# Index-add over 32 batches: one staged batch behind each of the first five groups, and shared DMA semaphores

## The chip, the cores and the metric

The kernel runs on one core of a Trainium2 chip. The metric is the device time of one execution in microseconds. Before the change it is 84.39 us, the median of 3 runs (83.99 to 84.44). A change of about 0.5% is what such runs can tell from none.

## The reference

For each of 32 batches, 128 rows of `source` are added to rows of `x` that `indices` names. An index can occur several times in a batch, and then all its rows are added.

```python
batch, seq, dim = 32, 512, 256          # x: 32 x 512 x 256, f32
num_updates = 128                       # indices: 32 x 128, source: 32 x 128 x 256
result = x.copy()
for b in range(batch):
    for i in range(num_updates):
        result[b, indices[b, i]] += source[b, i]
```

## The kernel before

The batches are treated in eight groups of four (`GB = 4`), and in two ways.

**Direct batches**, 0 to 24. The whole batch of `x` is copied from HBM to HBM into `out` (`copy`, L117; four copies are issued by ScalarE, 21 by SyncE). GpSimd gathers the 128 rows of `x` that the indices name into `got` (`gather`, L459). TensorE multiplies the source rows by a matrix that says which updates have equal indices (`same`), so that each of the 128 rows of `add` in PSUM holds the full sum for its index (`sums`, L380 and L389). VectorE adds this to the gathered rows (L400), and GpSimd scatters them over the copy in `out` (`scatter`, L473). So that a repeated index is written once, `masks` (L288 to L361) works out for each update whether an earlier one has the same index; `to_i` (L361) is the row to write, or a number out of bounds, which the scatter skips. Gathers from batch 12 on (`SKIP_FROM`) also use `to_i`, and wait for it; the first twelve use `row_i`, which is ready earlier.

**Staged batches**, 25 to 31. The batch of `x` is loaded into SBUF (`load_x`, L136). In `staged_batch` VectorE makes a one-hot matrix (L407), TensorE spreads the source rows over all 512 rows of the batch in two halves (L421), VectorE adds each half to the loaded rows (L431), and SyncE stores the whole batch (L493).

**What sets the order.** Nothing is scheduled by a planner: each engine runs its instructions in the order in which they are written, and waits on semaphores. VectorE and TensorE get their work from one loop, which alternates `sums(g)`, `masks(g + 4)` and, from g = 2 on, one staged batch, after `masks(0)` to `masks(3)`:

```python
        for g in range(NG):
            sums(g)
            if g + MASKS_AHEAD < NG:
                masks(g + MASKS_AHEAD)
            if g >= 2:
                staged_batch(later.pop(0))
```

The staged batches are taken in the order 28, 29, 30, 31, 25, 26, 27. Groups 0 to 5 multiply in blocks of 32 rows, 16 matmuls a group; group 6 has one direct batch, and group 7 none, so `sums(7)` does nothing. A staged batch is two one-hot halves of two matmuls each. The profile counts every f32 matmul as two, so it shows 32 for a group's sums and 8 for a staged batch. `add` is a single buffer in PSUM, so `sums(g)` on TensorE waits for VectorE's L400 of the group before; `bc` and `spread` have two buffers each.

GpSimd's queue holds all 25 gathers in the order of batches, and behind them all 25 scatters in the same order. SyncE's queue holds the loads and copies in one fixed mixture (`LOADS`, `SRC_ORDER`), and behind them the seven stores, each waiting for its batch. Then it waits for all stores and all scatters, and the kernel ends.

**Semaphores.** Every direct batch has one for its copy (`s_copy`, waited for by its scatter) and one for its gather (`s_got`, waited for by the L400 of its group, four waits in a row).

Of the kernel before, what the change touches and what calls it, by code (L numbers as in the profile page):

```python
# [10 lines left out]
GB = 4  # L11
COPY_ROWS = 32
WIDE = 6
STAGED = (25, 26, 27, 28, 29, 30, 31)
MASKS_AHEAD = 4
SKIP_FROM = 12
# [3 lines left out]
def kernel(  # L20
# [18 lines left out]
    _, NU = indices.shape  # L39
# [3 lines left out]
    R = P // GB  # L43
    DIRECT = [b for b in range(B) if b not in STAGED]
    N_DIRECT = len(DIRECT)
    assert DIRECT[: WIDE * GB] == list(range(WIDE * GB))

# [14 lines left out]
    ident = sb.tile([B, B], f32)  # L62
    ident_r = sb.tile([B, WIDE * GB, R], f32)
    of_group = sb.tile([B, NG], f32)
# [14 lines left out]
    src = [sb.tile([P, GB, D], f32, name=f"src{g}") for g in range(NG)]  # L79
    got = [sb.tile([P, GB, D], f32, name=f"got{g}") for g in range(WIDE + 1)]  # L80
    same = [sb.tile([P, GB, P], f32, name=f"same{g}") for g in range(NG)]
    same_n = [sb.tile([P, GB, P], f32, name=f"same_n{k}") for k in range(2)]
    earlier = [sb.tile([P, GB, P], f32, name=f"earlier{k}") for k in range(2)]
    staged = {b: sb.tile([P, CH, D], f32, name=f"staged{b}") for b in STAGED}
    onehot = [sb.tile([P, CH, P], f32, name=f"onehot{k}") for k in range(2)]
# [8 lines left out]

    s_idx = tc.alloc_semaphore("s_idx")
    s_src = [tc.alloc_semaphore(f"s_src{g}") for g in range(NG)]
    s_copy = {b: tc.alloc_semaphore(f"s_copy{b}") for b in DIRECT}
    s_got = {b: tc.alloc_semaphore(f"s_got{b}") for b in DIRECT}
    s_in = {b: tc.alloc_semaphore(f"s_in{b}") for b in STAGED}
    s_out = tc.alloc_semaphore("s_out")  # L100
    s_store = tc.alloc_semaphore("s_store")
# [3 lines left out]
    def mark(name, ins):  # L105
        ins.then_inc(sems[name], 1)
        done[name] += 1
        return done[name]

    V, T, G = nc.vector, nc.tensor, nc.gpsimd  # L110

    with tc.tile_critical(no_gpsimd_drain=True):
# [10 lines left out]
        def load_src(g):  # L123
            rows = source[g * GB : (g + 1) * GB]
            if g < WIDE:
                nc.sync.dma_start(
# [19 lines left out]
        for n in range(N_DIRECT):  # L146
# [3 lines left out]
            if n in LOADS:  # L150
# [28 lines left out]
                out=ident_r[:, :, :],  # L179
                in_=ident[:, : WIDE * GB].unsqueeze(2).to_broadcast([B, WIDE * GB, R]),  # L180
            ),
        )


        for g in range(SKIP_FROM // GB, WIDE + 1):
            k_zero = mark("act", nc.scalar.memzero(got[g][:, :, :]))  # L186
# [180 lines left out]
        def sums(g):  # L367

            here = [b for b in range(g * GB, (g + 1) * GB) if b in DIRECT]
            if not here:  # L370
                return
            T.wait_ge(s_src[g], 16)
            T.wait_ge(sems["dve"], max(k_same[g], k_idx_w, *k_sum.values()))
            if g < WIDE:
                for c in range(GB):
                    for e in range(GB):
                        rows = slice(R * e, R * (e + 1))
                        k = mark(
                            "pe",
                            T.matmul(  # L380
                                out=add[:, e, :D], lhsT=same[g][rows, c, :],
                                rhs=src[g][rows, c, :], start=c == 0, stop=c == GB - 1,
                            ),
                        )
            else:
                for b in here:
                    k = mark(
                        "pe",
                        T.matmul(  # L389
                            out=add[:, b % GB, :D], lhsT=same[g][:, b % GB, :],  # L390
                            rhs=src[g][:, b % GB, :], start=True, stop=True,
                        ),
                    )
            V.wait_ge(sems["pe"], k)
            for b in here:
                V.wait_ge(s_got[b], 16)
            rows = got[g][:, : len(here), :]
            k_sum[g] = mark(
                "dve",
                V.tensor_tensor(out=rows, in0=rows, in1=add[:, : len(here), :D], op=Alu.add),  # L400
            )

        def staged_batch(b):
            i = len(k_staged)
            k_hot = mark(
                "dve",
                V.tensor_scalar(  # L407
                    out=onehot[i % 2][:, :, :], in0=place_f[:, :, :],
                    scalar1=idx_f[:, b : b + 1], scalar2=None, op0=Alu.is_equal,
                ),  # L410
            )
            for half in range(2):
                n = len(k_spread)
                T.wait_ge(s_src[b // GB], 16)
                T.wait_ge(sems["dve"], k_hot)
                if n >= N_SP:
                    T.wait_ge(sems["dve"], k_spread[n - N_SP])
                for c in range(2):
                    k = mark(
                        "pe",  # L420
                        T.matmul(  # L421
                            out=spread[n % N_SP][:, c, :], lhsT=onehot[i % 2][:, 2 * half + c, :],
                            rhs=src[b // GB][:, b % GB, :], start=True, stop=True,
                        ),
                    )
                V.wait_ge(sems["pe"], k)
                V.wait_ge(s_in[b], 16)
                rows = staged[b][:, 2 * half : 2 * half + 2, :]
                k_spread[n] = mark(
                    "dve",  # L430
                    V.tensor_tensor(  # L431
                        out=rows, in0=rows, in1=spread[n % N_SP][:, :, :], op=Alu.add
                    ),
                )
            k_staged[b] = k_spread[n]
# [2 lines left out]
            masks(g)  # L438
        ORDER = [28, 29, 30, 31, 25, 26, 27]
        later = list(ORDER)  # L440
        for g in range(NG):
            sums(g)
            if g + MASKS_AHEAD < NG:
                masks(g + MASKS_AHEAD)
            if g >= 2:
                staged_batch(later.pop(0))
        for b in later:
            staged_batch(b)
# [2 lines left out]
        def gather(n):  # L451
            b = DIRECT[n]

            skips = n >= SKIP_FROM
            if n == SKIP_FROM:
                G.wait_ge(sems["act"], k_zero)
            if skips:
                G.wait_ge(sems["dve"], k_to[b // GB])
            G.indirect_dma_start(  # L459
                out=got[b // GB][:, b % GB, :],  # L460
                out_offset=None,
                in_=x_rows,
                in_offset=bass.IndirectOffsetOnAxis(
                    ap=(to_i if skips else row_i)[:, b : b + 1], axis=0
                ),
                **(dict(bounds_check=last_row, oob_is_err=False) if skips else {}),
            ).then_inc(s_got[b], 16)

        def scatter(n):
            b = DIRECT[n]  # L470
            G.wait_ge(s_copy[b], 16)
            G.wait_ge(sems["dve"], max(k_sum[b // GB], k_to[b // GB]))
            G.indirect_dma_start(  # L473
                out=out_rows,
                out_offset=bass.IndirectOffsetOnAxis(ap=to_i[:, b : b + 1], axis=0),
                in_=got[b // GB][:, b % GB, :],
                in_offset=None,
                bounds_check=last_row,
                oob_is_err=False,
            ).then_inc(s_out, 16)  # L480
# [3 lines left out]
        for n in range(N_DIRECT):  # L484
            gather(n)
        for n in range(N_DIRECT):
            scatter(n)
# [8 lines left out]

        nc.sync.wait_ge(s_store, 16 * len(STAGED))
        nc.sync.wait_ge(s_out, 16 * N_DIRECT)
# [30 lines left out]
```

## Time and profile before

| | |
|---|---|
| median of 3 runs | 84.39 us (83.99 to 84.44) |
| the profiled execution, its own time | 83.16 us |
| its span, first to last instruction | 81.4 us |
| granted TensorE clock, mean | 0.876 |
| busy: TensorE, VectorE, GpSimd, ScalarE | 53.3, 44.1, 50.6, 5.9 us |
| bytes moved by DMA | 30.71 MB, mean 377 GB/s |
| DMA queue share: SyncE, GpSimd, ScalarE | 68.1%, 18.9%, 6.3% |

All details come from this one execution; it was 83.16 us long, of which 1.76 us lie around the span. In lists of instructions the first number is the start in us from the span's start, the second the duration. PE is TensorE, DVE is VectorE, POOL is GpSimd, SP is SyncE; a group of instructions stands as line, engine, operation and `out<-in`. What is in square brackets is how long the engine had been idle and what ended that. In lists of waits, the three numbers are microseconds in total, how many waits, and the longest.

### The profile page before, as it was taken

To read this page: it belongs to the slowest core of one execution; us is meant where nothing else is said; L and a number is where in the kernel's file an instruction comes from. 1 tells how busy PE (TensorE), PEld (TensorE's weight loads), DVE (VectorE), ACT (ScalarE), POOL (GpSimd) and SP (SyncE) were. 2 spreads that over 40 slices of the span, in tenths; PEclk is the share of its full clock that TensorE was granted. 3 is DMA by queue.
4 is the path that set the end of the run, shared out by engine and by line. 5 is a ranking of instruction groups with operands and counts; after the bars stand their busy time and mean duration, and the time that the engine had idled before them with its cause. 6 is when DMAs were issued, how large, how long until landed. Compare 5 with 4: busy or idle time off the path is not lost.

```text
span 81.4 us, 998 instructions
## 1 busy us (share of the span) xinstructions
PE 53.3 (66%) x335; PEld 43.9 (54%) x335; DVE 44.1 (54%) x80; ACT 5.9 (7%) x6; POOL 50.6 (62%) x59
## 2 busy tenths in 40 slices
PE   0119989999999976049990399369909954945000
PEld 0019967799999884048690368165707651733000
DVE  1480399999399499943329642534171548356000
ACT  0299600000000000000000000000000000000000
POOL 4187877874378787877868787787868778600000
PEclk9999999999999999855599965985895699999975
DMA  0799989999999999999999999999999999999810
GB/s 2 284 373 439 409 325 426 421 395 453 423 419 384 443 428 391 404 458 414 384 363 429 439 382 411 466 425 383 446 413 408 423 393 415 413 414 402 352 46 0
DMA packets 7588, 30.71 MB, mean 377 GB/s; under 512 B 1568, under 2 KB 2637, under 8 KB 6784
## 3 DMA queue, kind: packets, MB, share of 16 engines
q1 hardware_dynamic: 4992, 22.58, 68.1%
q0 software_dynamic: 2400, 5.99, 18.9%
q10 hardware_dynamic: 192, 2.10, 6.3%
q8 instruction: 2, 0.03, 0.2%
q14 instruction: 2, 0.02, 0.0%
HBM read 24.28 MB, written 20.05 MB: 545 GB/s over the span
## 4 chain that ended last, share of the span: by engine, by line
PE 55%; DVE 22%; issue 13%; DMA 2%; SPq 0%; DVEq 0%
PE spread L421 23%; PE add L380 19%; PE bc L301 7%; DVE earlier L345 3%; DVE dup L353 3%; DVE got L400 3%; DVE same_n L332 2%; PE add L261 2%; PE bc L288 2%; DVE same L320 2%; DMA idx_raw<-in_indices_dram 2%; DVE onehot L407 2%; DVE idx_by_place L249 1%; DVE staged L431 1%; DVE place_f L241 1%
## 5 line engine op out<-in xcount | busy, mean ns | idle before, releaser
L473 POOL DMA_INDIRECT out_dram<-got,to_i x25 | 24.7, 988 | 7.7 <-issue 6.4
L421 PE MATMUL spread<-src,onehot 128*128 128x256 f32 x56 | 18.5, 488 | 14.4 <-issue 8.0
L421 PEld LDWEIGHTS spread<-src,onehot 128*128 128x128 f32 x56 | 12.6, 236 | 18.6 <-issue 16.6
L380 PE MATMUL add<-src,same 32*128 32x256 f32 x192 | 18.4, 531 | 0.4 <-DVE got L400 0.4
L431 DVE TENSOR_TENSOR staged<-staged,spread 128x512 f32<-128x512 f32 x14 | 9.6, 688 | 14.7 <-PE spread L421 14.7
L459 POOL DMA_INDIRECT got<-in_x_dram,to_i x13 | 13.0, 999 | 6.2 <-DVE to_i L361 2.5
L380 PEld LDWEIGHTS add<-src,same 32*128 32x128 f32 x192 | 14.7, 274 | 3.4 <-issue 1.9
L459 POOL DMA_INDIRECT got<-in_x_dram,row_i x12 | 12.1, 1006 | 5.3 <-issue 3.3
L301 PE MATMUL bc<-idx_bt,ident 32*128 32x128 f32 x64 | 13.2, 369 | 0.4 <-DVE same_n L332 0.4
L400 DVE TENSOR_TENSOR got<-got,add 128x1024 f32<-128x1024 f32 (+1 forms) x7 | 7.7, 1106 | 8.9 <-PE add L380 8.8
L301 PEld LDWEIGHTS bc<-idx_bt,ident 32*128 32x128 f32 x64 | 12.0, 272 | 1.0 <-DVE same_n L332 0.7
L353 DVE TENSOR_REDUCE dup<-earlier 128x4 f32<-128x512 f32 x8 | 5.5, 686 | 0.3
L332 DVE TENSOR_TENSOR same_n<-bc,idx_f 128x512 f32<-128x512 f32 x6 | 4.1, 689 | 1.1 <-PE bc L301 1.1
L320 DVE TENSOR_TENSOR same<-bc,idx_w 128x512 f32<-128x512 f32 x6 | 4.1, 684 | 0.5 <-PE bc L288 0.5
L345 DVE TENSOR_TENSOR earlier<-same_n,before 128x512 f32<-128x512 f32 x6 | 4.2, 692 | 0.2
L288 PE MATMUL bc<-idx_bt,ident_r 32*128 32x128 f32 x12 | 4.0, 430 | 0.3 <-DVE same L320 0.3
L186 ACT ACTIVATE got<-got 128x1024 uint32<-128x1024 uint32 x4 | 3.9, 1042 | 0.0
L288 PEld LDWEIGHTS bc<-idx_bt,ident_r 32*128 32x128 f32 x12 | 3.2, 304 | 1.3 <-DVE same L320 0.9
L261 PE MATMUL add<-of_group,idx_by_place 32*128 32x8 f32 x8 | 1.9, 358 | 2.5 <-DVE idx_by_place L249 2.5
L407 DVE TENSOR_SCALAR onehot<-place_f,idx_f 128x512 f32<-128x512 f32 x7 | 3.4, 479 | 0.0
L261 PEld LDWEIGHTS add<-of_group,idx_by_place 32*128 32x128 f32 x8 | 1.8, 324 | 2.6 <-DVE idx_by_place L249 2.6
L215 PE MATMUL add<-ident,idx_bt 32*128 32x32 f32 x1 | 0.3, 282 | 3.0 <-DVE idx_bt L208 3.0
(28 smaller groups left out, 12.7 us busy)
## 6 DMA issues: line engine op xcount, KB each, us to landing
out_dram<-in_x_dram SPq DMA_DIRECT2D x21, 512.0 KB, 20.0
src<-in_source_dram SPq DMA_DIRECT2D x8, 512.0 KB, 18.8
staged<-in_x_dram SPq DMA_DIRECT2D x7, 512.0 KB, 20.8
out_dram<-staged SPq DMA_DIRECT2D x7, 512.0 KB, 8.8
out_dram<-in_x_dram ACTq DMA_DIRECT2D x4, 512.0 KB, 7.7
out_dram<-got,to_i POOLq DMA_INDIRECT x25
got<-in_x_dram,to_i POOLq DMA_INDIRECT x13, 7.1
got<-in_x_dram,row_i POOLq DMA_INDIRECT x12, 6.8
```

Of the source, the lines that this page charges most:

```text
L288: T.matmul(out=bc[n % N_BC][:, 0, :], lhsT=ident_r[:, g * GB : (g + 1) * GB, :].rearrange("b e p -> b (e p)"), rhs=idx_bt[:, :], start=Tru ...
L301: T.matmul(out=bc[n % N_BC][:, e, :], lhsT=ident[:, b : b + 1].to_broadcast([B, P]), rhs=idx_bt[:, :], start=True, stop=True,),
L320: V.tensor_tensor(out=same[g][:, :, :], in0=ps[:, 0, :].unsqueeze(1).to_broadcast([P, GB, P]), in1=idx_w[:, :, g].unsqueeze(2).to_broadcas ...
L332: V.tensor_tensor(out=shared[:, :, :], in0=ps[:, :, :], in1=idx_f[:, gs].unsqueeze(2).to_broadcast([P, GB, P]), op=Alu.is_equal,),
L345: V.tensor_tensor(out=earlier[g % 2][:, :, :], in0=shared[:, :, :], in1=before[:, :].unsqueeze(1).to_broadcast([P, GB, P]), op=Alu.mult,),
L353: V.tensor_reduce(out=dup[:, gs], in_=earlier[g % 2][:, :, :], op=Alu.max, axis=X),
L380: T.matmul(out=add[:, e, :D], lhsT=same[g][rows, c, :], rhs=src[g][rows, c, :], start=c == 0, stop=c == GB - 1,),
L400: V.tensor_tensor(out=rows, in0=rows, in1=add[:, : len(here), :D], op=Alu.add),
L421: T.matmul(out=spread[n % N_SP][:, c, :], lhsT=onehot[i % 2][:, 2 * half + c, :], rhs=src[b // GB][:, b % GB, :], start=True, stop=True,),
L431: V.tensor_tensor(out=rows, in0=rows, in1=spread[n % N_SP][:, :, :], op=Alu.add),
L459: G.indirect_dma_start(out=got[b // GB][:, b % GB, :], out_offset=None, in_=x_rows, in_offset=bass.IndirectOffsetOnAxis(ap=(to_i if skips ...
L473: G.indirect_dma_start(out=out_rows, out_offset=bass.IndirectOffsetOnAxis(ap=to_i[:, b : b + 1], axis=0), in_=got[b // GB][:, b % GB, :], ...
```

## The change

Three things are changed. `staged_by` says how many staged batches follow the sums and masks of each group: one behind groups 0 to 4, none behind 5 to 7. The remaining two are done after the loop. The order of the batches is the same.

The gathers of a group share one semaphore, and the group's L400 waits once for all of them. The copies of batches 0 to 11 (`COPY_GROUPS = 3`) share one semaphore for each group of four, and a scatter of such a batch waits until all four copies have landed. Later copies keep a semaphore each. The queues of GpSimd, SyncE and ScalarE hold the same instructions in the same order as before; in the changed file the lines lie a few further down (L361 becomes L367, L421 L426, L431 L436, L493 L499).

```diff
+COPY_GROUPS = 3
...
-    s_copy = {b: tc.alloc_semaphore(f"s_copy{b}") for b in DIRECT}
-    s_got = {b: tc.alloc_semaphore(f"s_got{b}") for b in DIRECT}
+
+    s_copy_g = [tc.alloc_semaphore(f"s_copy_g{g}") for g in range(COPY_GROUPS)]
+    s_copy = {
+        b: s_copy_g[b // GB] if b < COPY_GROUPS * GB else tc.alloc_semaphore(f"s_copy{b}")
+        for b in DIRECT
+    }
+    s_got = [tc.alloc_semaphore(f"s_got{g}") for g in range(WIDE + 1)]
...
             V.wait_ge(sems["pe"], k)
-            for b in here:
-                V.wait_ge(s_got[b], 16)
+            V.wait_ge(s_got[g], 16 * len(here))
...
+        staged_by = {0: 1, 1: 1, 2: 1, 3: 1, 4: 1}
         for g in range(NG):
             sums(g)
             if g + MASKS_AHEAD < NG:
                 masks(g + MASKS_AHEAD)
-            if g >= 2:
+            for _ in range(staged_by.get(g, 0)):
                 staged_batch(later.pop(0))
         for b in later:
             staged_batch(b)
...
-            ).then_inc(s_got[b], 16)
+            ).then_inc(s_got[b // GB], 16)
...
-            G.wait_ge(s_copy[b], 16)
+            G.wait_ge(s_copy[b], 16 * GB if b < COPY_GROUPS * GB else 16)
```

## The prediction

> **What bounds the kernel now.** I read the page's slices first, for how full the DMA engines are.
>
> ```profile
> DVE  1480399999399499943329642534171548356000
> POOL 4187877874378787877868787787868778600000
> DMA  0799989999999999999999999999999999999810
> ```
>
> DMA is full from about 3 to 75 us: 16 engines working off one pile of bytes, which the change leaves as it is. Work done earlier is worth something only where the engines run dry. Two questions remain: what is issued last, and what may slip before it becomes the last. The groups of waits on SP and the timelines of SP and POOL tell the first.
>
> ```profile
> SPq L493 <- DVE staged L431: 18.2, 6, 7.6
> SPq L112 <- DMA out_dram<-staged: 3.7, 1, 3.7
> ```
>
> SP waits for the seven staged batches before storing them, and at the very end 3.7 us for a store, not for a scatter. The last store goes out at 75.1 (tile staged: 47.5 to 75.1). A look at the DMA traffic by window finds none after 79.2, and the span ends at 81.4: 2.2 us behind the last traffic. POOL's queue shows none after 75.5, so the scatters have 79.2 - 75.5 = 3.7 us to spare. In 75 to 76 the DMA share is 0.68, the one hole.
>
> POOL's timeline (start, duration) is the second chain: 25 gathers, then 25 scatters, strictly in that order.
>
> ```profile
> 32.19 1.00 POOL L459 DMA_INDIRECT got<-in_x_dram,to_i  x1 [0.30 <-issue]
> ...
> 37.40 1.00 POOL L459 DMA_INDIRECT got<-in_x_dram,to_i  x1 [0.30 <-issue]
> 38.70 1.03 POOL L473 DMA_INDIRECT out_dram<-got,to_i  x1 [0.30 <-DVE staged L431]
> ...
> 69.80 0.98 POOL L473 DMA_INDIRECT out_dram<-got,to_i  x1 [0.36 <-DMA out_dram<-in_x_dram]
> ```
>
> Gather 20 starts at 32.19 and gather 24 at 37.40, one each 1.30 us; the first scatter at 38.70, the last at 69.80, one each 1.29 us. POOL has no reserve: an issue delayed at the gathers delays all scatters. Gathers 20 to 23 need `to_i` of group 5, gather 24 that of group 6. VectorE's timeline has them:
>
> ```profile
> 26.34 0.16 DVE L361 SCALAR_TENSOR_TENSOR to_i<-dup,row_f 128x4 int32<-128x4 f32 x1
> 27.53 1.22 DVE L400 TENSOR_TENSOR got<-got,add 128x1024 f32<-128x1024 f32 x1 [1.02 <-PE add L380]
> ...
> 31.43 0.16 DVE L361 SCALAR_TENSOR_TENSOR to_i<-dup,row_f 128x4 int32<-128x4 f32 x1
> 31.64 1.22 DVE L400 TENSOR_TENSOR got<-got,add 128x1024 f32<-128x1024 f32 x1
> ...
> 34.97 0.16 DVE L361 SCALAR_TENSOR_TENSOR to_i<-dup,row_f 128x4 int32<-128x4 f32 x1
> 35.05 0.48 DVE L407 TENSOR_SCALAR onehot<-place_f,idx_f 128x512 f32<-128x512 f32 x1
> ```
>
> Group 5's `to_i` is ready at 31.59, group 6's at 35.13; gather 24 at 37.40 has 2.3 us to spare, gather 20 only 0.6. The first staged batch starts behind both, at 35.05.
>
> **The change part by part.** *Batch 28 moves in front of sums(1), batch 29 in front of sums(2).* Before, TensorE computed sums(1) while VectorE did masks(4), and both stretches were nearly full. Now TensorE's queue has batch 28's spread in front of sums(1), and that waits for a one-hot that VectorE makes only after masks(4). What one spread and the sums behind it take together, TensorE's timeline shows three times:
>
> ```profile
> 35.67 3.75 PE L421 MATMUL spread<-src,onehot 128*128 128x256 f32 x8 [3.93 <-DVE onehot L407]
> 39.35 2.65 PE L380 MATMUL add<-src,same 32*128 32x256 f32 x32
> ...
> 46.12 2.39 PE L421 MATMUL spread<-src,onehot 128*128 128x256 f32 x8 [3.24 <-issue]
> 48.44 3.22 PE L380 MATMUL add<-src,same 32*128 32x256 f32 x32
> ...
> 53.53 2.96 PE L421 MATMUL spread<-src,onehot 128*128 128x256 f32 x8 [1.88 <-issue]
> 56.42 2.65 PE L380 MATMUL add<-src,same 32*128 32x256 f32 x32
> ```
>
> From the spread's start to the L400 behind its sums: 35.67 to 42.16, 46.12 to 51.81, 53.53 to 59.23, or 6.49, 5.69 and 5.70, mean 5.96. At the full clock throughout it would be 1.97 (the spread at 66.03) + 2.01 (the sums at 28.89) + 0.15 = 4.13; at half clock throughout, 3.75 + 4.0 + 0.15 = 7.9. I take 5.96, since here too TensorE has idled before each block, as before those three; the half-clock end is kept for the first block, because until 27 the sums of this trace ran at half speed (29 matmuls in 3.62 us).
>
> Replayed from 26.42, when VectorE is through with masks(4):
> - one-hot 28, 0.48, and 0.1 to TensorE: the spread starts at 27.00. Block 5.96: L400(1) at 32.96 (was 27.53).
> - L400(1) to group 5's `to_i`: 31.59 - 27.53 = 4.06, ready at 37.02 (was 31.59, +5.4).
> - one-hot 29 starts 0.08 before that end, 0.48 and 0.1: spread at 37.52, L400(2) at 43.48; to group 6's `to_i` 35.13 - 31.64 = 3.49, ready at 46.97 (was 35.13, +11.8).
> - The batches' four updates at L431 (0.69 each) add nothing here: TensorE is still in the sums. Batch 28's rows of x are in SBUF at 20.1 and 29's at 29.1 by their semaphores; each is needed later.
>
> *POOL behind it.* Gather 20 goes at about 37.4, four of them to 42.6; gather 24 waits for 46.97. From `to_i` to the gather took 0.29 after L219 (3.55 to 3.84) and 0.79 for gather 12 (20.96 to 21.75); I take 0.5, so 47.5, +10.1. The scatters follow at their pace, and the last starts at 69.80 + 10.1 = 79.9. Their other waits are over: group 5's sums end at 72.3 by the replay below, and scatter 20 starts at 74.7.
>
> *From the last scatter to the end.* Loaded, the last scatter took 5.7 us from start to last traffic. No scatter here ran on idle DMA engines. Ends: 4.5, the quickest store's issue to landing, and 5.7; I take 5.2, nearer the scatter's own row. Traffic ends at 85.1, the span 2.2 later at 87.3: +5.9.
>
> The row is that 5.7. The Trainium skill, "DMA: Bandwidth & Descriptors", section "Anatomy of one DMA — SWDGE (gpsimd) path", gives about 2.0 us fixed plus the bytes over 436 GB/s, so an estimated 2.3 for one scatter of 128 KB. By that figure the sum would be +3.0. The trace's gathers (6.0 at the least to landing) speak against it.
>
> *What is taken off the tail.* Three batches followed sums(6); now two. A batch there costs 71.82 - 68.63 = 3.19, hidden under DMA traffic until 75. Replay of VectorE from 46.89: batch 30 and sums(3) to L400(3) at 53.43; 3.39 (42.16 to 45.55) to one-hot 31, L400(4) at 63.36; 1.14 to one-hot 25, L400(5) at 71.04, written at 72.3; sums(6) by 73.5; batches 26 and 27, 3.19 + 3.28, to 80.0. So VectorE too ends 4.9 later than at 75.1: two batches saved at the tail are paid at 6.5 and more in front, where they break up an overlap. The last store's traffic, 2.4 (most engines at 77.5) to 4.1 (the last at 79.2) behind its issue, ends at 82.4 to 84.1, just under the scatters' 85.1.
>
> *Shared semaphores.* A group's sums wait once instead of four times; the waits cost VectorE's queue 0.05 each where seen, mostly while it waits for TensorE: 0 to -0.2 on the path, taken as 0. Scatters 0 to 11 wait for all four copies of their group. The last copy of group 2 landed at 35.8 by its semaphore, group 2's first scatter ran at 49.08: 0, with 13 us of cover.
>
> Of these shared counts a row says only that those copies had all landed long before. The Trainium skill, "DMA: Bandwidth & Descriptors", section "Why a DMA increments its semaphore by 16 and not by 1", advises one semaphore per transfer in flight, as a partial count tells nothing; by it a scatter pays the slowest copy of four, which this order of issue makes nothing.
>
> **The sum.** +5.9 on 81.4 is a span of 87.3; with the 1.76 that the profiled execution has around its span (83.16 - 81.4), 89.1. The profiled execution was 1.2 below the median of the runs shown. The forecast stands on that median: 84.39 + 5.9 = 90.3.
>
> **The rivals.**
> 1. *The stores end it.* If the scatters slip less than the replay has it, the last store at about 80.0 decides: traffic to 82.4 to 84.1, span +3.2 to +4.9, 87.6 to 89.3. For it: the two chains are 1.0 to 2.7 apart. Against: whatever delays VectorE delays both.
> 2. *The full clock in both blocks*, 4.13 each: 3.7 off, 86.6. Against: none of three blocks had it.
> 3. *Not slower: the scatters' reserve covers it.* The reserve decides: POOL may be 3.7 us late before the scatters outlast the stores' old end, that is gather 24 at 41.1, group 6's `to_i` at 40.6. The DMA engines then end the kernel, and the earlier stores fill the hole at 75 to 76, 0.32 us: 84.1 to 84.4. It needs 6.4 less than the replay's 46.97, blocks of 2.8 each, below even the 4.13 of a full clock.
>
> **How the numbers follow.** Forecast (scatters last) 0.78, rival 1 0.11, rival 2 0.05, rival 3 0.06. Forecast alone: low, blocks of 5.0 (between 4.13 and 5.69), wake 0.3 and tail 4.5, -2.8: 87.5; high, a first block of 7.9 and a second of 6.49 less the mean (+2.5), wake 0.8 and tail 5.7 (+0.8): 93.6, rarely all together, so 92.9. With rival 1, and with the profiled execution's 89.1 as a centre, the low end is 86.9. The kernel's measurement tells 0.5% (0.4 us) from no change. Rivals 1, 2 and the forecast are slower: 0.94; rival 3 splits evenly, 0.03 same and 0.03 faster.
>
> **What will show it.** POOL's timeline: gather 20 near 37.4, gather 24 near 47.5 with a wait for L367 (`to_i`) ahead of each, first scatter near 48.8, last near 79.9. TensorE's: an idle stretch near 24 to 27, then spread and sums in turn. VectorE's last L436 near 80. SP's last wait for scatters rather than stores. DMA slices falling off well before the end. Wrong if gather 24 starts before 41, if TensorE's two blocks take 3 us each, or if the scatters' pace falls below 1.29.

## The result, and the profile after

The changed kernel takes 87.81 us (median of 8 runs, 87.03 to 89.76), the kernel before 84.06 in the same comparison (8 runs, 83.05 to 84.44). The ratio is 1.0447, with a 95% interval of 1.0397 to 1.0498. The forecast was 90.3, or +5.9; it came to about +3.8. Some executions of a kernel fall into a slower state of the chip: medians here are over all executions and ratios over those outside it, and in the comparison whose median before is 83.85 only two of the seven lie outside, so its ratios stand on little.

The profiled execution of the changed kernel was the longest of the eight (89.76, span 87.8), with an index load 0.75 us slower than before's, so its places are read as late by about that, and its total is not set against before's. The spans of the five shortest executions lie between 85.2 and 86.1. The page's slices of the changed kernel, for VectorE, GpSimd and DMA:

```profile
DVE  1290399998594332972329460881506335464300
POOL 4077877781678770027700487787777778778400
DMA  0999999999999999999999999999999968217450
```

GpSimd has two holes (about 33 to 39 and 44 to 49 us), which it did not have, and its work reaches to the end; DMA is no longer full from the 33rd slice on (about 70 us). GpSimd's timeline shows what made the holes:

```profile
38.87 1.00 POOL L465 DMA_INDIRECT got<-in_x_dram,to_i  x1 [6.15 <-DVE to_i L367]
...
49.19 1.00 POOL L465 DMA_INDIRECT got<-in_x_dram,to_i  x1 [5.42 <-DVE to_i L367]
50.49 1.03 POOL L479 DMA_INDIRECT out_dram<-got,to_i  x1 [0.30 <-issue]
...
81.49 0.98 POOL L479 DMA_INDIRECT out_dram<-got,to_i  x1 [0.30 <-issue]
```

Gather 20 waited 6.15 us and gather 24 5.42 us, both for `to_i`, and the last scatter starts at 81.49 where it was 69.80. TensorE's timeline has the two blocks, each behind an idle stretch:

```profile
27.54 3.75 PE L426 MATMUL spread<-src,onehot 128*128 128x256 f32 x8 [3.31 <-DVE onehot L412]
31.22 3.17 PE L386 MATMUL add<-src,same 32*128 32x256 f32 x32
...
39.10 3.75 PE L426 MATMUL spread<-src,onehot 128*128 128x256 f32 x8 [3.61 <-issue]
42.79 2.51 PE L386 MATMUL add<-src,same 32*128 32x256 f32 x32
```

From spread to L405 they took 7.00 (27.54 to 34.54) and 6.36 (39.10 to 45.46). Both spreads took 3.75 us, at a granted clock of 0.50 throughout.

SP's waits at the end have one line that was not there before, the last of these:

```profile
SPq L504 <- DMA out_dram<-got,to_i: 1.2, 1, 1.2
SPq L118 <- DMA out_dram<-staged: 1.2, 1, 1.2
SPq L118 <- POOLq L118: 1.2, 1, 1.2
```

SP waits for the scatters' landing, then 1.2 us more for the last store, then another 1.2 for GpSimd itself. In this profile the last store's traffic ends at 84.7, 1.2 behind the scatters' 83.5. So after the result two theories were open: the forecast's, that the scatters' chain on GpSimd decides, and rival 1, that the last store does. I leaned to rival 1. What GpSimd still had to do after its last scatter, neither said.

### The profile page after: what moved, and what is told of

Same layout as the page of the kernel before. It is cut to its first block, busy times and chain, and to the rows that moved or that the text cites. A ratio compares the mean times of both kernels' runs of the same rounds, so it can differ in the third digit from the quotient of the medians.

```text
span 87.8 us, 992 instructions
## 1 busy us (share of the span) xinstructions
PE 55.2 (63%) x335; PEld 43.8 (50%) x335; DVE 44.5 (51%) x80; ACT 5.9 (7%) x6; POOL 50.7 (58%) x59
## 2 busy tenths in 40 slices
DMA packets 7588, 30.71 MB, mean 350 GB/s; under 512 B 1568, under 2 KB 2637, under 8 KB 6784
## 4 chain that ended last, share of the span: by engine, by line
PE 51%; issue 17%; DVE 17%; POOL 4%; DMA 3%; POOLq 2%; SPq 0%
PE spread L426 20%; PE add L386 20%; PE bc L307 7%; POOL out_dram L479 4%; DVE got L405 3%; DMA idx_raw<-in_indices_dram 3%; DVE earlier L351 2%; DVE dup L359 2%; DVE same_n L338 2%; PE add L267 2%; DVE same L326 2%; PE bc L294 2%; POOLq L494 2%; DVE onehot L412 1%; DVE idx_by_place L255 1%
## 5 line engine op out<-in xcount | busy, mean ns | idle before, releaser
L426 PE MATMUL spread<-src,onehot 128*128 128x256 f32 x56 | 21.1, 543 | 17.8 <-issue 13.3
L426 PEld LDWEIGHTS spread<-src,onehot 128*128 128x128 f32 x56 | 14.3, 268 | 22.2 <-issue 19.6
L465 POOL DMA_INDIRECT got<-in_x_dram,to_i x13 | 13.1, 1004 | 17.1 <-DVE to_i L367 14.1
L436 DVE TENSOR_TENSOR staged<-staged,spread 128x512 f32<-128x512 f32 x14 | 9.6, 687 | 17.4 <-PE spread L426 17.4
L386 PE MATMUL add<-src,same 32*128 32x256 f32 x192 | 17.7, 519 | 0.0
L386 PEld LDWEIGHTS add<-src,same 32*128 32x128 f32 x192 | 13.6, 269 | 4.7 <-issue 3.3
L405 DVE TENSOR_TENSOR got<-got,add 128x1024 f32<-128x1024 f32 (+1 forms) x7 | 7.8, 1108 | 12.5 <-PE add L386 11.7
L307 PE MATMUL bc<-idx_bt,ident 32*128 32x128 f32 x64 | 12.5, 354 | 0.4 <-DVE same_n L338 0.4
L307 PEld LDWEIGHTS bc<-idx_bt,ident 32*128 32x128 f32 x64 | 11.5, 261 | 1.0 <-DVE same_n L338 0.7
```

What stands on the lines that cost most here:

```text
L307: T.matmul(out=bc[n % N_BC][:, e, :], lhsT=ident[:, b : b + 1].to_broadcast([B, P]), rhs=idx_bt[:, :], start=True, stop=True,),
L386: T.matmul(out=add[:, e, :D], lhsT=same[g][rows, c, :], rhs=src[g][rows, c, :], start=c == 0, stop=c == GB - 1,),
L426: T.matmul(out=spread[n % N_SP][:, c, :], lhsT=onehot[i % 2][:, 2 * half + c, :], rhs=src[b // GB][:, b % GB, :], start=True, stop=True,),
L436: V.tensor_tensor(out=rows, in0=rows, in1=spread[n % N_SP][:, :, :], op=Alu.add),
L465: G.indirect_dma_start(out=got[b // GB][:, b % GB, :], out_offset=None, in_=x_rows, in_offset=bass.IndirectOffsetOnAxis(ap=(to_i if skips ...
```

## The experiments

**The parts apart.** First the order without the shared semaphores, then the semaphores without the order.

```diff
 # the kernel before, and only this
+        staged_by = {0: 1, 1: 1, 2: 1, 3: 1, 4: 1}
...
-            if g >= 2:
+            for _ in range(staged_by.get(g, 0)):
                 staged_batch(later.pop(0))
```

> The staged batches in the new order, every semaphore as before the change. If the order alone makes the loss, this is the changed kernel again: 87.0 to 88.0 us, gather 20 near 38, gather 24 near 48, last store issued near 82. If the shared semaphores had a part in it, it is nearer to the 84.1 of before, by as much as they cost. My theory: 87.6, within 0.4 of the changed kernel.

Measured: 88.33 us (88.04 to 88.75) against 83.64, ratio 1.0558 (1.0496 to 1.062). Gather 20 started at 37.53, gather 24 at 47.19, the last scatter at 79.93, close to the replay's 37.4, 47.5 and 79.9; the time is 0.7 above the 87.6 expected, and so outside the 0.4 allowed. SP's waits at its end, and the drain that the code gives GpSimd behind its last scatter (duration in ns three times, then its start):

```profile
SPq L499 <- DMA out_dram<-got,to_i: 2.8, 1, 2.8
SPq L112 <- POOLq L112: 1.9, 1, 1.9
```

```profile
L489 POOLq DRAIN  x1: 14107/14107/14107, 71.0 to 71.0; - x1
```

There is no wait for a store: the scatters end it, and behind them the drain, at 71.0 + 14.1 = 85.1. The last scatter itself ended at 80.91, so the drain runs on for 4.16.

```diff
 # the changed kernel, with the order of before
-        staged_by = {0: 1, 1: 1, 2: 1, 3: 1, 4: 1}
...
-            for _ in range(staged_by.get(g, 0)):
+            if g >= 2:
                 staged_batch(later.pop(0))
```

> The order of before, with the shared semaphores alone. Theory that the order makes the whole loss: 84.1, the time of before within 0.4. Rival, the shared semaphores cost a wait: up to a few us slower, with a scatter or a sum of groups 0 to 2 later than before. At the very end the clearing of the semaphores, 0.46 us before and 0.31 in the changed kernel, should be 0.31: up to 0.15 us less, too little for the time to show.

Measured: 83.28 us (83.13 to 84.01) against 83.85; ratio 1.0102, interval 0.9943 to 1.0261, though the median is the lower one, so no difference is shown. The order makes the loss. The clearing of the semaphores at the end did shrink, from 461 ns before to 312 ns with the semaphores shared.

**GpSimd's delay alone.** The kernel before, in which one gather waits longer and nothing else is touched.

```diff
-                G.wait_ge(sems["dve"], k_to[b // GB])
+                G.wait_ge(sems["dve"], k_to[7] if n == N_DIRECT - 1 else k_to[b // GB])
```

> The kernel before, whose gather 24 alone waits for to_i of group 7 (near 45.6) in place of group 6's; TensorE, VectorE and the stores are as before. Gather 24 near 46.0, 8.6 late, the last scatter started near 78.4. Theory that GpSimd's delay alone makes the loss: the end follows the last scatter's start by the 6.4 of the runs with a late GpSimd, a span near 84.9, 86.5 to 87.5 us. Rival, the stores or VectorE's longer chain made the loss: these are untouched here, so 83.7 to 84.8.

Measured: 85.91 us (85.73 to 87.33) against 83.85; ratio 1.0398 (1.0232 to 1.0564). GpSimd's timeline, SP's last wait and the drain:

```profile
44.07 1.00 POOL L459 DMA_INDIRECT got<-in_x_dram,to_i  x1 [5.89 <-DVE to_i L361]
...
76.36 0.98 POOL L473 DMA_INDIRECT out_dram<-got,to_i  x1 [0.30 <-issue]
```

```profile
SPq L112 <- POOLq L112: 1.6, 1, 1.6
```

```profile
L488 POOLq DRAIN  x1: 14194/14194/14194, 68.4 to 68.4; - x1
```

Group 7's `to_i` came earlier than I had it, at 43.8, and the delay was smaller; the time stayed 0.6 below the expected range. Still, with the programs of TensorE, VectorE and the stores as before, a late GpSimd alone makes the kernel slower: its shortest execution, 85.73, is above the longest of the kernel before in this comparison, 85.19. And the program ends 1.4 us behind its drain (82.6, span 83.9).

**GpSimd's delay taken away, the batches left early.** The changed kernel, with the masks that the gathers wait for done ahead of the first staged batch.

```diff
-            if g + MASKS_AHEAD < NG:
-                masks(g + MASKS_AHEAD)
+            for m in {0: (4, 5, 6), 3: (7,)}.get(g, ()):
+                masks(m)
```

> The changed kernel with masks(5) and masks(6) done right behind masks(4), so that to_i of groups 5 and 6 is ready before the first staged batch and GpSimd is not held up: gather 24 near 38, last scatter near 70 as before the change. VectorE and TensorE have the same work in the same alternation, so the last store still goes out near 82. Theory that the last store decides the end: no gain, 87.0 to 88.0. Rival, the scatters decide (the forecast): the delay of 11 us at GpSimd is gone and the time falls to what the stores allow, by the forecast's own distance of 1.0 to 2.7, to 84.9 to 86.6.

Measured: 84.52 us (84.29 to 84.89) against 83.64; ratio 1.0103 (1.0043 to 1.0163). Of the 5.6% that the order alone lost in the same comparison 1.0% is left. My leaning to the stores would have had no gain. The scatters are not quite back where they were (GpSimd's timeline, and SP's last wait):

```profile
70.54 1.01 POOL L479 DMA_INDIRECT out_dram<-got,to_i  x1 [2.55 <-DVE got L405]
...
75.78 0.98 POOL L479 DMA_INDIRECT out_dram<-got,to_i  x1 [0.30 <-issue]
```

```profile
SPq L118 <- POOLq L118: 0.5, 1, 0.5
```

Scatter 20 waits 2.55 us for its group's sums, and scatter 16 had waited 3.06; both start 0.78 behind the end of their group's sums, which VectorE writes late because the staged batches stand in front. The last store goes out at 77.4, SP waits 1.2 for it, and then 0.5 more for GpSimd. So GpSimd is still the last, by little, and what holds it now is the longer chain of VectorE and TensorE; with `masks(7)` out as well ("Both", below) those two waits are gone.

**The stores' chain shortened, GpSimd's left late.** The changed kernel without `masks(7)`. That leaves out the search for duplicates in group 7, whose result nothing uses.

```diff
-            if g + MASKS_AHEAD < NG:
+            if g + MASKS_AHEAD < NG - 1:
                 masks(g + MASKS_AHEAD)
```

> The changed kernel without masks(7), whose to_i nothing reads (group 7 has only staged batches). It takes 3.45 - 1.14 = 2.3 us out of VectorE's path behind the fourth group's sums, and nothing out of GpSimd's. Theory that the last store decides: it is issued near 80 in place of 82.3, its traffic ends near 82.4, and then the scatters' 83.5 decide: 1.2 less, about 86.4. Rival, the scatters decide: nothing moves, 87.0 to 88.0.

Measured: 88.56 us (87.72 to 89.22) against 83.64; ratio 1.0548 (1.0467 to 1.0629). Nothing gained: the order alone took 88.33 in the same comparison. The lines of the stores' issue, of the drain, and of SP's last two waits:

```profile
L499 SPq DMA_DIRECT2D out_dram<-staged x7: 332/332/1117, 45.4 to 75.3; - x7
```

```profile
L494 POOLq DRAIN  x1: 15838/15838/15838, 68.9 to 68.9; - x1
```

```profile
SPq L504 <- DMA out_dram<-got,to_i: 6.3, 1, 6.3
SPq L118 <- POOLq L118: 2.3, 1, 2.3
```

The last store is issued at 75.3, 7.0 earlier than in the changed kernel's profile, and the time stays. (The missing search is 2.3 of that by the expectation; the two profiles also differ in TensorE's mean granted clock, 0.898 here and 0.827 there.) Rival 1 falls with this run: SP's waits end with the scatters' landing and then the drain, which ends at 68.9 + 15.8 = 84.7, and no wait ends with a store, whose traffic is over by 78.8.

**Both.**

```diff
-            if g + MASKS_AHEAD < NG:
-                masks(g + MASKS_AHEAD)
+            for m in {0: (4, 5, 6)}.get(g, ()):
+                masks(m)
```

> Both: masks(5) and masks(6) behind masks(4), and no masks(7). The scatters end near 76 and the last store is issued near 80. Theory that the last store decides: its whole 2.3 us come off, about 85.3. Rival, the scatters decide: as with the masks early, no more than that one gains.

Measured: 83.83 us (83.36 to 84.72) against 83.64; ratio 0.9998 (0.9926 to 1.0071): the time of before. The stores' line and SP's last wait:

```profile
L499 SPq DMA_DIRECT2D out_dram<-staged x7: 332/333/2582, 46.1 to 69.6; - x7
```

```profile
SPq L118 <- DMA out_dram<-staged: 3.2, 1, 3.2
```

The last store is issued at 69.6, where before issued it at 75.1: 5.5 us earlier, and the span is 81.6 against 81.4. (Other profiles with the order of before issue it at 72.0 to 73.2, so 75.1 is late among them.) With both delays taken out, the earlier stores bring nothing that shows. A store that is issued earlier only stands longer in a full queue: from issue to landing the stores took 21.6 us in the median, where it was 8.8 before.

**What the full queue is worth.** The same kernel without its last store, so that `out[27]` is not written.

```diff
-        for b in ORDER:
+        for b in ORDER[:-1]:
             nc.sync.wait_ge(sems["dve"], k_staged[b])
...
-        nc.sync.wait_ge(s_store, 16 * len(STAGED))
+        nc.sync.wait_ge(s_store, 16 * (len(STAGED) - 1))
```

> The kernel with masks early and no masks(7), whose time was that of before, without the last store: out[27] is not written. Its last store was issued at 69.6 where before issued it at 75.1, and the span did not move. Theory that the bytes are the floor: 0.52 MB less at 400 GB/s take off 1.3 us, about 82.5 us (no more, since GpSimd's drain at 78.8 comes next). Rival, the end is set by something else, a landing time or the engines' end: no change, 83.5 to 84.2.

Measured: 82.34 us (81.30 to 83.22) against 83.86; ratio 0.981 (0.9713 to 0.9907). 0.52 MB less took off about 1.5 us, where 1.3 was expected of the bytes. Together with the run before it, this says that the bytes set the time of before; but the run also takes away the transfer that lands last, and the two are not told apart.

**The drain.** The kernel with the late gather 24, without the drain behind the last scatter.

```diff
         for n in range(N_DIRECT):
             scatter(n)
-        G.drain()
```

> The same late gather 24, without the drain that GpSimd is given behind its last scatter. In the runs with a late GpSimd that drain ends 4.16 us behind the last scatter's own end and 2.4 to 2.8 behind the landing that SyncE waits for, and SyncE's last wait is for GpSimd. Theory that the drain is the last link: the end moves up to the landing, some 2.3 us less than with the late gather and the drain. Rival, the drain at the very end of the program takes its place, or the landing decides: no change.

Measured: 88.29 us (87.69 to 88.78), 2.4 more than with the drain (85.91, in the same comparison); ratio to before 1.0705 (1.0549 to 1.0862). Neither expectation held. The closing drains of GpSimd at the program's end (shortest, median, longest in ns; first and last start):

```profile
L523 POOLq DRAIN  x3: 40/177/4148, 80.3 to 85.4; - x3
```

One of them now takes 4.15 us, and it starts at 80.3, only after SP has seen everything landed. The rival was right in that the end drain takes the place, but it is worse: the drain in the code had run beside the landing.

**How large GpSimd's reserve is.** Two runs delay gather 24 by a little: one by moving only one batch in front of `masks(6)` and none in front of `masks(5)`, the other in the kernel before by the wait alone.

```diff
 # the changed kernel
-        staged_by = {0: 1, 1: 1, 2: 1, 3: 1, 4: 1}
+        staged_by = {1: 1, 2: 1, 3: 1, 4: 1, 5: 1}
```

> The changed kernel with staged batches behind groups 1 to 5 in place of 0 to 4: only one is ahead of masks(6), none ahead of masks(5). to_i of group 6 then comes near 40.5 in place of 35.1 and 47 to 49, gather 24 near 40.8, the last scatter near 73.3. Theory that GpSimd's delay makes the loss, and that it has a reserve of some 3.7 us or more: all of this is inside the reserve, 83.7 to 84.5, no loss. Rival, the broken overlap of TensorE and VectorE costs in proportion to the batches moved: half of the 4, about 86.

Measured: 84.52 us (83.92 to 84.88) against 83.85; ratio 1.0244 (1.0138 to 1.0349). Gather 24 started at 40.66, the last scatter at 73.05, as expected. By the medians it cost 0.7; the ratio's larger loss rests on two executions of the kernel before, so that it cost something is likely, and how much is open. The drain ended at 80.9 and the last store was issued at 75.8, 0.7 later than before; SP waited 1.3 for that store and 0.3 for GpSimd. Most of the loss of the full change is gone with one batch in place of two.

```diff
 # the kernel before
-                G.wait_ge(sems["dve"], k_to[b // GB])
+                G.wait_ge(sems["dve"], k_spread[1] if n == N_DIRECT - 1 else k_to[b // GB])
```

> The kernel before, whose gather 24 waits for the first staged batch's second update (near 40.2), 3.0 late; TensorE, VectorE and the stores as before. The last scatter starts near 72.8. The forecast's reserve of 3.7 us counted the scatters' traffic alone: by it nothing is lost, 83.3 to 84.3. Theory that the drain is the last link: GpSimd's drain ended at 77.98 before, and SyncE was ready for it at 79.9, so the reserve is 1.9; the drain would end near 81.0 and the time rise by about 1.1.

Measured: 83.78 us (83.31 to 84.54, 12 runs) against 83.86; ratio 1.0034 (0.9995 to 1.0074). Gather 24 at 39.80 in a run whose index load was 0.66 late, so it was delayed by only 1.7. The drain:

```profile
L488 POOLq DRAIN  x1: 11054/11054/11054, 69.7 to 69.7; - x1
```

It ended at 80.7, just as SP was ready for it. The delay came out too small to tell a reserve of 1.9 from one of 3.7 by the time.

**The changed kernel again.**

> The changed kernel again, for a second profile beside the first, whose index load came 0.75 us later than before's. 87.0 to 88.3; gather 24 near 47 to 48, the last scatter started near 80, the span's end 6.3 to 6.5 behind that start.

Measured: 89.33 us (88.05 to 90.15) against 83.86; ratio 1.0589 (1.0504 to 1.0674). That is above the expected 87.0 to 88.3, and its interval lies just above that of the first comparison (1.0397 to 1.0498): the loss is 3.75 us there, 4.9 by the ratio or 5.5 by the medians here, and so is known to a microsecond or two only. In its profile gather 24 starts at 49.0 and the last scatter at 81.4, again with an index load that late. SP waits 2.6 for the scatters and then 1.6 for GpSimd, and for no store; the end follows the last scatter's start by 6.6.

**A kernel that may be better.** Masks early, no `masks(7)`, and two more steps.

```diff
 # on top of "both"
-STAGED = (25, 26, 27, 28, 29, 30, 31)
+STAGED = (26, 27, 28, 29, 30, 31)
-SKIP_FROM = 12
+SKIP_FROM = 20
...
-        LOADS = {5 + 3 * i: b for i, b in enumerate((28, 29, 30, 31, 25, 26, 27))}
+        LOADS = {5 + 3 * i: b for i, b in enumerate((28, 29, 30, 31, 26, 27))}
...
-        ORDER = [28, 29, 30, 31, 25, 26, 27]
+        ORDER = [28, 29, 30, 31, 26, 27]
```

> An attempt at a better kernel: masks early, no masks(7), batch 25 direct in place of staged, and gathers up to batch 19 by row_i, without a wait for to_i. A direct batch moves 0.52 + 0.13 + 0.12 MB, a staged one 1.05, so 0.28 less; the duplicates of two more groups are fetched, about 0.12 more: 0.16 MB or 0.4 us less by the bytes. GpSimd has one gather and one scatter more (2.6) and starts its last gathers about 3 us earlier. Theory that the bytes are the floor: 0.4 less than before, 83.2 to 83.6. Rival, GpSimd's chain: 1 us or more above.

Measured: 83.37 us (82.52 to 84.23, 12 runs) against 83.86 (23 runs); ratio 0.9954, interval 0.9909 to 0.9999. It moved 30.54 MB in place of 30.71, and the gain of 0.4 us is the size that the bytes give. The interval just leaves out 1, so I would call it a small gain that wants more runs.

## Why the prediction was right, and where not

The direction and the mechanism held, step by step. Batches 28 and 29 broke the overlap of TensorE's sums with VectorE's masks; `to_i` of groups 5 and 6 came late; the gathers and all scatters behind them slipped. The last scatter started at 79.9 (the order alone), 81.4 and 81.5 (the two profiles of the change, with an index load late by about 0.8), against 79.9 in the replay. The late gather alone made the kernel slower, the early masks removed most of the loss.

The size was too large by 2.1 (5.9 against 3.75) in the first comparison, and by 0.4 to 1.0 in the second. The step that failed is *From the last scatter to the end*: 5.2 + 2.2 = 7.4 was forecast; from the last scatter's start to the end of the span it was 6.34 in the changed kernel (81.49 to 87.83) and 6.6 when it was run again, 6.34 without `masks(7)`, 6.5 with the order alone. Both of its terms were wrong, in opposite directions, and that they nearly cancel is luck. The last scatter's traffic took 2.0 in place of 5.2 (81.49 to 83.5), with the DMA engines busy for 0.45 of that time, where they were full behind before's last scatter; in the second profile of the change it took 2.9, at 0.66. I had kept the range between 4.5 and 5.7, and the true value lay outside it. The page of the Trainium skill that I had weighed against the trace, "DMA: Bandwidth & Descriptors", section "Anatomy of one DMA — SWDGE (gpsimd) path", with an estimated 2.3, was near for this last scatter, which landed 2.4 behind its start. Scatters in the changed kernel land 2.4 to 6.7 behind their issue, so it does not hold for all of them:

```profile
DMA to landing us min/median/max: 2.4/5.2/6.7
```

And the end is not 2.2 behind the traffic but behind GpSimd's drain, which I had not looked at. In the changed kernel it is this line, and ends at 77.0 + 9.6 = 86.6:

```profile
L494 POOLq DRAIN  x1: 9580/9580/9580, 77.0 to 77.0; - x1
```

That is 4.16 behind the last scatter's end at 82.47, and the span ends 1.2 later. The rest of the first comparison's excess, about 1.1, is not in one term: 0.5 is the base, since the span that I added to (81.4) was at the short end of the kernel before (81.3 to 82.5 in the comparison with the order alone); and about 0.5 the start of the last scatter, if 6.34 is taken off the five shortest spans of the change (85.2 to 86.1, so 78.9 to 79.8). That last number is inferred, as those executions have no profile here.

*The block of 5.96* held as a middle: 7.00 and 6.36 in the change's profile, 6.54 and 5.69 with the order alone, 5.56 and 5.62 without `masks(7)`. It varies by over 1 us with where TensorE's clock falls: the second blocks, 6.36, 5.69 and 5.62, had a granted clock of 0.63, 0.70 and 0.72. The slow sums before 27, which the prediction took for half speed, have a granted clock of 1.00 beside them, but the trace holds no clock record ahead of 27.05; so what slowed them is not shown.

*Rival 1* looked right in the profile after, and was wrong: the last store can be issued 7 us earlier without any gain. *Rival 3* was right that earlier stores are worth nothing or next to it (ratio 0.9998 when only they are left), but its reserve of 3.7 counted the scatters' traffic. By the drain it was 1.9: before, the drain ended at 69.6 + 8.4 = 78.0, and SP came to wait for it at 79.9.

```profile
L488 POOLq DRAIN  x1: 8418/8418/8418, 69.6 to 69.6; - x1
```

That is read from one profile; no time here tells a reserve of 1.9 from one of 3.7. A delay of gather 24 by 3.3, from one moved batch, left SP waiting 0.3 for GpSimd.

*Shared semaphores at 0* held: no wait showed, and the clearing at the end took 0.15 us less, which the forecast did not have.

## What to carry to other kernels

Before moving work forward, look for what is queued behind it on the other engines: here two instructions that write `to_i`, each 0.16 us long, stood in front of 25 scatters of 1.29 us each, and the reserve of that chain, not the work moved, decided the price. In this kernel, whose DMA engines are full almost to the end, an earlier store bought nothing, and fewer bytes did. And measure a chain's reserve to its last instruction, its drain included, and not to its last traffic.

## What was not expected of the hardware

GpSimd's drain behind indirect DMAs has two lower bounds in these profiles. It ends 4.16 us behind the last scatter's own end (80.91 to 85.07, 80.56 to 84.72, 82.47 to 86.63) or 2.07 behind the landing that SP sees (75.91 to 77.98 before, 80.49 to 82.56 with the late gather, 78.65 to 80.72 with the little delay), whichever is later. Left out of the code, 4.15 us come back at the program's end, where nothing hides them.

From its start to its last packet, the last scatter took 5.7 to 5.9 us in the six profiles in which the DMA engines were full meanwhile (a share of 0.97 or more), 5.4 in one with 0.87, and 2.0 to 3.7 in the seven in which their share was 0.30 to 0.79. Its 128 KB alone would be 0.3 us by an estimate at the 400 GB/s that the engines move here when full.
